# Products of the probabilities with v in 512 columns, once per head and sequence, from one generation of transposed probabilities

## The chip, the core and the metric

The kernel runs on one core of a Trainium2 chip. A core has a matrix engine (TensorE, "PE" in the profile; its loads of stationary operands are shown apart as "PEld"), a vector engine ("DVE"), a scalar engine ("ACT"), a general engine ("POOL") and a sync engine ("SP") that issues the DMAs between device memory and on-chip memory. On-chip memory is SBUF (operands) and PSUM (banks of 128 x 512 32-bit numbers, into which TensorE writes). Each engine works off its own list of instructions in order, and waits on semaphores for the others. The metric is the time of one execution in microseconds (us) on the device; lower is better. A result is the median of several runs.

## The reference, cut to what matters

An encoder layer over two sequences of 512 tokens (a "prompt" and a "sample"), with 1024 features. Three branches stand beside each other (a state-space scan, a differential attention, a cross attention to a memory), then gated merging, and a feed-forward part. The change lies in the differential attention. It has four heads; each head has two softmax maps over the same 512 keys, and their difference weights v:

```python
def _diff_attention(q, k, v, lam, subln_g, lambda_init):
    ...
    def block(qblk):
        s = jnp.einsum('bqhd,bkhd->bhqk', qblk, k).astype(jnp.float32) * scale
        probs = jax.nn.softmax(s, axis=-1).reshape(Bn, DIFF_HEADS, 2, Q_BLOCK, L)
        w = probs[:, :, 0] - lam * probs[:, :, 1]
        return jnp.einsum('bhqk,bkhe->bqhe', w.astype(v.dtype), v)

    o = lax.map(block, qb)
    o = o.transpose(1, 0, 2, 3, 4).reshape(Bn, L, DIFF_HEADS, DIFF_VDH)
    o = _rmsnorm(o, subln_g) * (1.0 - lambda_init)
    return o.reshape(Bn, L, DIFF_WIDTH)
```

All of it is in 32-bit floating point.

## The kernel before, in words

**Halves.** A product of two 32-bit matrices is made from reduced-precision halves: `split` (lines 131 to 139) writes the high half with a copy on ACT (line 134 or 137) and the low half, the remainder, on DVE (line 135 or 138). A product then takes three matmuls: high by high, low by high, high by low.

**The attention phase** (lines 736 to 940) goes through 32 steps. A step is a head h (0 to 3), a sequence s (0 or 1) and a block qt of 128 queries (0 to 3), in this nesting, so four steps in a row share h and s. The loop (lines 919 to 933) has an index i; its iteration i does, in the order in which TensorE gets it:

- if i is odd, `scores(i + 1)`: the two maps of steps i+1 and i+2. For each of the two steps, six matmuls on TensorE make two banks; DVE takes the row maxima (line 543, tile `nb`), ACT the exponentials (line 548, tile `e`), and DVE combines the two maps into `e0` (lines 552, 864, 865);
- `fill(10)`: some ten matmuls of other work (filler, below);
- `turn(i)`: TensorE transposes the four 128 x 128 blocks of `e0` into one bank of the pool `tr` (line 875; line 69 in the profile, `bktr<-ident,e`), ACT writes the high half `pH` (line 134), DVE the low half `pL` (line 135);
- if step i-1 has an odd qt, `outputs(i - 1)`: the product of v with the transposed probabilities of two query blocks, 12 matmuls of 256 columns into one half of a bank of the pool `oo` (lines 891 to 893). After the second half of a head and sequence, ACT copies the bank to `osb` (line 896);
- `fill(10)` again;
- two iterations after the last block of a head and sequence, `squares`: TensorE transposes `osb`, ACT squares and sums rows (line 907); three iterations after it, `normed`: `factor` takes a root on ACT (line 198) and a reciprocal on DVE (line 199, tile `rs`), TensorE spreads the factors (line 202; line 69 in the profile, `bktr<-ident,rs`), DVE scales `osb` (line 915) and SP stores it.

Below, "turn k" is the call of `turn` for step k, and "outputs k" the call of `outputs` that follows step k.

**Filler.** `fill` takes units from a queue of generators: projections of the layer's input to q, k, v and gates (tiles `xh`, `xl`, `wh`, `wl`), and towards the end the products of the merging (`yh`, `yl`). Their banks (pool `mm`, two of them) are emptied by DVE (lines 752 and 754 for q and k, line 797 for the merging), or by ACT (line 632 for gates). The gates are stored to device memory (`gD`) and loaded again (`gl`); the other branches' outputs come from `bD` into `yt`, and are split into `yh` and `yl`.

**Buffers.** The pool `tr` has two PSUM banks, shared in turn by one bank of `scores`, by `turn`, by `squares` and by `normed`; the pool `sc` has three, the pool `oo` one. `pT` has four slots of 128 x 4 x 256: two generations of `pH` and `pL`, each for two query blocks.

**What sets the order.** On TensorE the attention phase keeps the order in which the code is written (`PE.on = True`, line 687). On the other engines the framework's scheduler places the instructions by its own estimates, so that a change in the code can move rows there too.

Of the kernel before, what the change touches and what calls it, by code (L numbers as in the profile page):

```python
# [10 lines left out]
F32 = mybir.dt.float32  # L11
F32R = mybir.dt.float32r
# [7 lines left out]
P = 128  # L20
L = 512
# [51 lines left out]
def encoder(ctx: ExitStack, tc: tile.TileContext, a, out):  # L73
    nc = tc.nc
    V, S, PO, PE = nc.vector, nc.scalar, nc.gpsimd, InOrder(tc, nc.tensor)
# [8 lines left out]
    rp = ctx.enter_context(tc.tile_pool(name="rp", bufs=2))  # L84
# [3 lines left out]
    def open_tags(es, side=None, **tags):  # L88

        for tag, n in tags.items():  # L90
            pools[tag] = es.enter_context(tc.tile_pool(name=tag, bufs=n, side=side, reuse_waits="tile"))
# [10 lines left out]
    xp_es, phase = ExitStack(), ExitStack()  # L102
# [3 lines left out]
    def slot(tag, shape=(P, NT), dt=F32, name="sl"):  # L106
        return pools[tag].tile(list(shape), dt, tag=tag, name=name)

    def bank(tag="mm"):
        return pools[tag].tile([P, 512], F32, tag=tag, name="bk" + tag)  # L110

    def aux():
        return bank("tr")
# [17 lines left out]
    def split(hi, lo, src, scale=None):  # L131

        if scale is None:
            h = S.copy(hi, src)  # L134
            l_ = V.tensor_tensor(out=lo, in0=src, in1=hi.bitcast(F32), op=ALU.subtract)  # L135
        else:
            h = S.activation(out=hi, in_=src, func=AF.Copy, scale=scale)
            l_ = V.scalar_tensor_tensor(out=lo, in0=src, scalar=scale, in1=hi.bitcast(F32), op0=ALU.mult, op1=ALU.subtract)
        return h, l_
# [210 lines left out]
    with yielding(last_s):  # L350
        x_norm(0, norm[0], range(5, 8))
        _, bc = factor(ss1, DM)
# [245 lines left out]
    def fill(n):  # L598
        nonlocal owed
        owed += n  # L600
        while owed > 0 and queue:
            r = next(queue[0], None)
            if r is None:
                queue.pop(0)
            else:
                owed -= r
        if not queue:
            owed = 0

    def finish(g):  # L610
        while any(g is g_ for g_ in queue):
            fill(1)
# [75 lines left out]
    steps = [(h, s, lt) for h in range(4) for s in range(NS) for lt in range(4)]  # L688
    es, pT = {}, {}
    AHEAD = 2  # L690
    for i in range(-AHEAD, len(steps) + 1):
        if i + AHEAD < len(steps):
            h, s, lt = steps[i + AHEAD]
# [12 lines left out]
        if 0 <= i < len(steps):  # L706
            h, s, lt = steps[i]
# [3 lines left out]
            tr = aux()  # L711
# [4 lines left out]
        if i > 0 and steps[i - 1][2] == 3:  # L716
            h, s, _ = steps[i - 1]
            pTh, pTl = pT.pop((h, s))
            oo = bank("oo")
# [5 lines left out]
            osb = xa.tile([P, L], F32, tag="osb", name="xosb", bufs=1)  # L725
# [7 lines left out]
    phase.close()  # L733


    open_tags(phase, v2=2, qk=12, pT=4)
    aes = ExitStack()
    ap_ = aes.enter_context(tc.tile_pool(name="att", bufs=2, reuse_waits="tile"))
    acol = aes.enter_context(tc.tile_pool(name="acol", bufs=2, reuse_waits="tile"))
# [21 lines left out]
    qk = {}  # L761
# [48 lines left out]
    def first_in():  # L810
        b0.append(merge_in(0, ["qk", "qk", "qk", "v"]))
        yield 0
# [31 lines left out]
    s0, ss, osb = {}, {}, {}  # L844
# [22 lines left out]

    def turn(i):
        h, s, qt = steps[i]
        if qt % 2 == 0:  # L870
            pT[h, s, qt // 2] = tuple(slot("pT", [P, 4, 2 * P], F32R, n_) for n_ in ("pH", "pL"))
        e0 = es.pop(i)
        tr = aux()
        for j in range(4):
            PE.transpose(tr[:, j * P : (j + 1) * P], e0[:, j * P : (j + 1) * P], ident)
        ps = slice(qt % 2 * P, qt % 2 * P + P)
        split(*(p_[:, :, ps] for p_ in pT[h, s, qt // 2]), tr.rearrange("p (j q) -> p j q", j=4))

    def outputs(i):

        h, s, qt = steps[i]
        if h == 2 and s == qt - 1 == 0:
            finish(v1_)
        vh, vl = (v1 if h >= 2 else v0)[s]
        vs = slice((h % 2) * P, (h % 2) * P + P)
        pH, pL = pT.pop((h, s, qt // 2))
        if qt == 1:
            osb[h, s] = bank("oo")
        od = osb[h, s][:, qt // 2 * 2 * P : (qt // 2 + 1) * 2 * P]
        for j in range(4):  # L890
            PE.matmul(od, vh[:, j, vs], pH[:, j, :], start=(j == 0), stop=False)
            PE.matmul(od, vh[:, j, vs], pL[:, j, :], start=False, stop=False)
            PE.matmul(od, vl[:, j, vs], pH[:, j, :], start=False, stop=(j == 3))
        if qt == 3:
            o_ = rp.tile([P, L], F32, tag="nsq", name="osb", bufs=2)
            S.copy(o_, osb[h, s])
            osb[h, s] = o_

    def squares(i):
        h, s, _ = steps[i]  # L900
# [17 lines left out]
    n = len(steps)  # L918
    for i in range(-1, n + 3):
        if i % 2 and i + 1 < n:  # L920
            scores(i + 1)
        if i == 22:
            queue.insert(1, first_in())
        fill(10 if i < n - 1 else 16)
        if 0 <= i < n:
            turn(i)
        if 0 < i <= n and steps[i - 1][2] % 2:
            outputs(i - 1)
        fill(10)
        if 1 < i <= n + 1 and steps[i - 2][2] == 3:  # L930
            squares(i - 2)
        if i > 2 and steps[i - 3][2] == 3:
            normed(i - 3)
# [218 lines left out]
    for i in range(KFF):  # L1152
# [14 lines left out]
        ps = products(i, w)  # L1167
        p0 = next(ps)
        if i == 0:
            for s in range(NS):  # L1170
                _, bc = rstd(accs[s], DM)
# [92 lines left out]
    for v, (m, lo_, hi_) in enumerate(VISITS):  # L1264
        ps = [bank() for _ in range(6)] + [aux()]
# [22 lines left out]
        ps = iter(ps)  # L1288
# [523 lines left out]
```

## Time and profile before

| what | value |
|---|---|
| median of 3 runs | 1598.01 us (1597.61 to 1598.38) |
| the profiled execution's own time | 1596.6 us |
| its span, first to last instruction | 1594.5 us |
| TensorE busy | 1576.7 us, 99% of the span, 7838 matmuls |
| DVE, ACT, POOL busy | 1161.4, 630.9, 531.5 us (73%, 40%, 33%) |
| attention phase, first to last turn | 529.36 to 744.42 us |
| matmuls of 128 x 256 in `outputs` | 192 (three groups of 64) |

A row of the timeline gives the start in us from the span's start, the duration in us, the engine, the line, the operation, the tiles written and read, and in brackets how long the engine had stood idle before it and for whom. Matmuls overlap: each shows a duration longer than the distance to the next, so the cost of one is the distance from its start to the next one's start. A line of the profile can be that of a helper: all matmuls show line 66, all transposes line 69, all high halves line 134 or 137 and all low halves line 135 or 138.

### The profile page before, as it was taken

How to read it: one execution, taken by the hardware profiler on the slowest of the kernel's cores; microseconds unless marked ns; L12 is line 12 of the kernel's file. 1: busy time of each engine (PE TensorE's matmuls, PEld its weight loads, DVE VectorE, ACT ScalarE, POOL GpSimd, SP SyncE). 2: the span in 40 equal slices, each digit the busy share in tenths (PEclk: the TensorE clock that was granted, in tenths of full speed). 3: DMA queues.
4: the chain of work that ended last, by engine and by line, in shares of the span. 5: the costliest groups of instructions: out<-in, count | busy, mean ns of one | idle time of the engine just before them, and what ended most of it. 6: DMA issues, size and time to landing. Idle time of an engine off the chain costs nothing.

```text
span 1594.5 us, 21527 instructions
## 1 busy us (share of the span) xinstructions
PE 1576.7 (99%) x7838; PEld 1316.7 (83%) x7838; DVE 1161.4 (73%) x1857; ACT 630.9 (40%) x1114; POOL 531.5 (33%) x434
## 2 busy tenths in 40 slices
PE   9999999999999999999999999999999999999997
PEld 7888888888898889878888888888888888788877
DVE  7978995076774766775545578888898778988664
ACT  6644213265552465573223443323333233233323
POOL 0010000001333221300443357666665553444553
PEclk9999999999999999999999999999999999999999
DMA  9553623675762111254543432333332223986222
GB/s 364 177 167 119 213 93 114 180 267 206 264 225 102 43 57 40 73 174 143 197 144 122 144 108 92 119 126 125 119 119 106 84 89 116 345 333 196 85 67 106
DMA packets 104890, 237.84 MB, mean 149 GB/s; under 512 B 13520, under 2 KB 45008, under 8 KB 104784
## 3 DMA queue, kind: packets, MB, share of 16 engines
q1 hardware_dynamic: 104784, 236.47, 43.6%
q8 instruction: 61, 1.00, 0.3%
q14 instruction: 45, 0.37, 0.1%
HBM read 165.16 MB, written 71.27 MB: 148 GB/s over the span
## 4 chain that ended last, share of the span: by engine, by line
PE 85%; DVE 5%; DMA 3%; issue 2%; POOL 2%; SPq 1%; ACT 1%; POOLq 0%; DVEq 0%; ACTq 0%
PE bkmm L66 74%; PE bktr L66 3%; PE bkoo L66 2%; DVE tl L135 2%; PE bktr L69 2%; PE bksc L66 1%; PE bktr L1646 1%; DMA wf<-in_w_in 0%; PE bktr L1583 0%; PE bktr L1707 0%; PE bktr L1706 0%; PE bktr L1705 0%; DVE wl L135 0%; SPq L1633 0%; DMA mt<-in_memT 0%
## 5 line engine op out<-in xcount | busy, mean ns | idle before, releaser
L66 PE MATMUL bkmm<-xh,wh 128*128 128x512 f32 x640 | 254.4, 398 | 0.0
L66 PE MATMUL bkmm<-xl,wh 128*128 128x512 f32 x640 | 250.3, 391 | 0.0
L66 PE MATMUL bkmm<-xh,wl 128*128 128x512 f32 x640 | 250.2, 391 | 0.0
L66 PE MATMUL bkmm<-th,wl 128*128 128x512 f32 (+1 forms) x621 | 241.1, 389 | 1.7 <-DVE wl L135 1.7
L66 PE MATMUL bkmm<-tl,wh 128*128 128x512 f32 (+1 forms) x621 | 241.0, 388 | 0.0
L66 PE MATMUL bkmm<-th,wh 128*128 128x512 f32 (+1 forms) x621 | 240.7, 388 | 0.0
L134 ACT CAST wh<-wf 128x1024 fp32r<-128x1024 f32 (+1 forms) x134 | 118.0, 880 | 211.2 <-PE bkmm L66 181.9
L135 DVE TENSOR_TENSOR wl<-wf,wh 128x1024 fp32r<-128x1024 f32 (+1 forms) x134 | 148.6, 1109 | 58.9 <-ACT wh L134 54.0
L66 PE MATMUL bkmm<-th,w 128*128 128x512 f32 x432 | 141.6, 392 | 3.3 <-DVE up L1119 1.5
L66 PEld LDWEIGHTS bkmm<-xh,wl 128*128 128x128 f32 x640 | 120.2, 188 | 26.3 <-issue 0.4
L66 PEld LDWEIGHTS bkmm<-xh,wh 128*128 128x128 f32 x640 | 120.3, 188 | 26.1 <-issue 3.2
L66 PEld LDWEIGHTS bkmm<-xl,wh 128*128 128x128 f32 x640 | 120.4, 188 | 22.3 <-issue 0.2
L66 PEld LDWEIGHTS bkmm<-th,wl 128*128 128x128 f32 x621 | 116.5, 188 | 26.5 <-DVE wl L135 2.7
L66 PEld LDWEIGHTS bkmm<-th,wh 128*128 128x128 f32 x621 | 116.6, 188 | 23.9
L66 PEld LDWEIGHTS bkmm<-tl,wh 128*128 128x128 f32 x621 | 116.6, 188 | 23.8
L454 POOL TENSOR_TENSOR raw<-raw 128x128 f32<-128x128 f32 x28 | 15.1, 540 | 307.0 <-DVE nb L545 228.9
L1183 POOL TENSOR_TENSOR up<-up,acc 128x512 f32<-128x512 f32 x44 | 84.1, 1930 | 84.2 <-DVE up L1119 84.2
L66 PEld LDWEIGHTS bkmm<-th,w 128*128 128x128 f32 x432 | 80.9, 188 | 24.9 <-DVE up L1119 4.8
L801 POOL TENSOR_TENSOR mg<-mg,gl 128x1024 f32<-128x1024 f32 x16 | 43.8, 2740 | 138.9 <-DVE gl L797 134.3
L66 PE MATMUL bkmm<-tl,w 128*128 128x512 f32 x216 | 84.2, 390 | 0.0
L1182 ACT ACTIVATE ac<-gf 128x512 f32<-128x512 f32 x44 | 27.8, 633 | 126.6 <-DMA aD<-ac 60.9
L66 PE MATMUL bkmm<-yh,wh 128*128 128x512 f32 x192 | 76.1, 396 | 0.0
(652 smaller groups left out, 3558.8 us busy)
## 6 DMA issues: line engine op xcount, KB each, us to landing
wf<-in_w_in SPq DMA_DIRECT2D x40, 512.0 KB, 3.8
wD<-hl SPq DMA_DIRECT2D x28, 512.0 KB, 2.9
w<-wD SPq DMA_DIRECT2D x28, 512.0 KB, 5.0
gD<-gt SPq DMA_DIRECT2D x24, 512.0 KB, 2.8
gl<-gD SPq DMA_DIRECT2D x24, 512.0 KB, 3.3
wf<-in_w_fg SPq DMA_DIRECT2D x22, 512.0 KB, 3.6
wf<-in_w_fu SPq DMA_DIRECT2D x22, 512.0 KB, 3.7
aD<-ac SPq DMA_DIRECT2D x22, 512.0 KB, 2.9
```

The lines of the kernel that those rows point to most:

```text
L66: return self.put(self.eng.matmul(*args, **kw))
L69: return self.put(self.eng.transpose(*args, **kw))
L134: h = S.copy(hi, src)
L135: l_ = V.tensor_tensor(out=lo, in0=src, in1=hi.bitcast(F32), op=ALU.subtract)
L454: PO.tensor_tensor(out=a22, in0=a21, in1=a22, op=ALU.add)
L801: PO.tensor_tensor(out=mg[m], in0=mg[m], in1=gt, op=ALU.add)
L1182: last_t = S.activation(out=ac[:, cs], in_=gf, func=AF.Tanh, scale=0.5)
L1183: PO.tensor_tensor(out=up, in0=up, in1=accs[s], op=ALU.mult)
L1646: PE.matmul(ps[:, g * P : (g + 1) * P], w_[:, gg * P : (gg + 1) * P], u_[:, 8 * o + gg, :], start=True, stop=True)
```

## The change

`pT` gets two slots instead of four, each twice as wide (128 x 4 x 512): one generation of `pH` and `pL`, for all four query blocks of a head and sequence. The same SBUF is taken: four slots of 4 x 256 columns against two of 4 x 512. `turn` writes its 128 columns of it. `outputs` is called once per head and sequence, after the fourth block, with 12 matmuls of 512 columns; the bank of `oo` is taken and copied in the same call. And `outputs(i - 1)` stands ahead of `turn(i)` in the loop, which means that TensorE reads all of `pH` and `pL` before it transposes the next first block, whose halves go into the same slots.

```diff
-    open_tags(phase, v2=2, qk=12, pT=4)
+    open_tags(phase, v2=2, qk=12, pT=2)
...
     def turn(i):
         h, s, qt = steps[i]
-        if qt % 2 == 0:
-            pT[h, s, qt // 2] = tuple(slot("pT", [P, 4, 2 * P], F32R, n_) for n_ in ("pH", "pL"))
+        if qt == 0:
+            pT[h, s] = tuple(slot("pT", [P, 4, L], F32R, n_) for n_ in ("pH", "pL"))
         e0 = es.pop(i)
         tr = aux()
         for j in range(4):
             PE.transpose(tr[:, j * P : (j + 1) * P], e0[:, j * P : (j + 1) * P], ident)
-        ps = slice(qt % 2 * P, qt % 2 * P + P)
-        split(*(p_[:, :, ps] for p_ in pT[h, s, qt // 2]), tr.rearrange("p (j q) -> p j q", j=4))
+        split(*(p_[:, :, qt * P : (qt + 1) * P] for p_ in pT[h, s]), tr.rearrange("p (j q) -> p j q", j=4))
 
     def outputs(i):
 
-        h, s, qt = steps[i]
-        if h == 2 and s == qt - 1 == 0:
+        h, s, _ = steps[i]
+        if h == 2 and s == 0:
             finish(v1_)
         vh, vl = (v1 if h >= 2 else v0)[s]
         vs = slice((h % 2) * P, (h % 2) * P + P)
-        pH, pL = pT.pop((h, s, qt // 2))
-        if qt == 1:
-            osb[h, s] = bank("oo")
-        od = osb[h, s][:, qt // 2 * 2 * P : (qt // 2 + 1) * 2 * P]
+        pH, pL = pT.pop((h, s))
+        od = bank("oo")
         for j in range(4):
             PE.matmul(od, vh[:, j, vs], pH[:, j, :], start=(j == 0), stop=False)
             PE.matmul(od, vh[:, j, vs], pL[:, j, :], start=False, stop=False)
             PE.matmul(od, vl[:, j, vs], pH[:, j, :], start=False, stop=(j == 3))
-        if qt == 3:
-            o_ = rp.tile([P, L], F32, tag="nsq", name="osb", bufs=2)
-            S.copy(o_, osb[h, s])
-            osb[h, s] = o_
+        osb[h, s] = rp.tile([P, L], F32, tag="nsq", name="osb", bufs=2)
+        S.copy(osb[h, s], od)
...
         fill(10 if i < n - 1 else 16)
+        if 0 < i <= n and steps[i - 1][2] == 3:
+            outputs(i - 1)
         if 0 <= i < n:
             turn(i)
-        if 0 < i <= n and steps[i - 1][2] % 2:
-            outputs(i - 1)
         fill(10)
```

In the built programs, TensorE's list is shorter by 96 matmuls, and POOL's order is the same. On DVE, ACT and SP all moved rows lie in the attention phase. Lines after 902 have numbers lower by five in the changed kernel (line 915 is line 910 there).

TensorE at iteration 12, where head 1 goes from its first sequence (steps 8 to 11) to its second, before: three matmuls of filler, the four transposes of turn 12 (`bktr<-ident,e`), then the first three of the twelve products of outputs 11.

```order
L66 MATMUL bkmm<-wh,xh_124 128x256
L66 MATMUL bkmm<-wl,xh_124 128x256
L66 MATMUL bkmm<-wh,xl_132 128x256
L69 MATMUL bktr<-ident,e 128x128 x4
L66 MATMUL bkoo<-pH,vh 128x256
L66 MATMUL bkoo<-pL,vh 128x256
L66 MATMUL bkoo<-pH,vl 128x256
```

The same place in the changed kernel: the last three of the twelve products of outputs 11, then the transposes, then filler.

```order
L66 MATMUL bkoo<-pH,vh 128x512
L66 MATMUL bkoo<-pL,vh 128x512
L66 MATMUL bkoo<-pH,vl 128x512
L69 MATMUL bktr<-ident,e 128x128 x4
L66 MATMUL bkmm<-wh,xh_125 128x256
L66 MATMUL bkmm<-wl,xh_125 128x256
L66 MATMUL bkmm<-wh,xl_133 128x256
```

The products have gone ahead of the transposes; the twelve products that followed turn 10 are gone, and stand here in the doubled width.

DVE at the same iteration, before: the rest of the score work of steps 12 and 13 around the low half `pL` of turn 11.

```order
L135 TENSOR_TENSOR rl<-t_6091,rh 128x512
L552 RECIPROCAL r<-sm 128x1
L864 SCALAR_TENSOR_TENSOR r<-r,nlam,s_6109 128x1
L865 SCALAR_TENSOR_TENSOR e<-e,r 128x512
L552 RECIPROCAL r<-sm 128x1
L864 SCALAR_TENSOR_TENSOR r<-r,nlam,s_6109 128x1
L135 TENSOR_TENSOR pL<-bktr,pH 128x4x128
L865 SCALAR_TENSOR_TENSOR e<-e,r 128x512
```

DVE there in the changed kernel:

```order
L552 RECIPROCAL r<-sm 128x1
L864 SCALAR_TENSOR_TENSOR r<-r,nlam,s_6066 128x1
L135 TENSOR_TENSOR rl<-t_6048,rh 128x512
L865 SCALAR_TENSOR_TENSOR e<-e,r 128x512
L135 TENSOR_TENSOR pL<-bktr,pH 128x4x128
L552 RECIPROCAL r<-sm 128x1
L864 SCALAR_TENSOR_TENSOR r<-r,nlam,s_6066 128x1
L865 SCALAR_TENSOR_TENSOR e<-e,r 128x512
```

`pL` of turn 11 has moved ahead of two small instructions of step 13.

DVE between iterations 26 and 27, before: low halves of the merging's inputs (`yl`), an emptying of a filler bank (line 797), and the scaling of `osb` of head 2's second sequence (line 915).

```order
L138 SCALAR_TENSOR_TENSOR yl_7430<-yt,yh_7429 128x1024
L138 SCALAR_TENSOR_TENSOR yl_7436<-yt,yh_7435 128x1024
L797 SCALAR_TENSOR_TENSOR mg_7326<-gl,bkmm 128x512
L138 SCALAR_TENSOR_TENSOR yl_7442<-yt,yh_7441 128x1024
L915 SCALAR_TENSOR_TENSOR osb<-osb,g_3468,bktr 128x512
L543 TENSOR_REDUCE nb<-bktr 128x1
```

DVE there in the changed kernel:

```order
L138 SCALAR_TENSOR_TENSOR yl_7331<-yt,yh_7330 128x1024
L797 SCALAR_TENSOR_TENSOR mg_7227<-gl,bkmm 128x512
L138 SCALAR_TENSOR_TENSOR yl_7337<-yt,yh_7336 128x1024
L910 SCALAR_TENSOR_TENSOR osb<-osb,g_3468,bktr 128x512
L543 TENSOR_REDUCE nb<-bktr 128x1
L138 SCALAR_TENSOR_TENSOR yl_7343<-yt,yh_7342 128x1024
```

The scaling of `osb` (and the first maximum of the next scores behind it) has moved ahead of the last `yl`, and the emptying ahead of the second.

## The prediction

> **What bounds the kernel now.** I read the page first, for which engine the end hangs on; then the busy time by stretches, for whether that holds in the attention phase too; then the waits of TensorE there; then the timeline around the products, for what a matmul really costs.
>
> ```profile
> span 1594.5 us, 21527 instructions
> PE 1576.7 (99%) x7838; PEld 1316.7 (83%) x7838; DVE 1161.4 (73%) x1857; ACT 630.9 (40%) x1114; POOL 531.5 (33%) x434
> ...
> PE 85%; DVE 5%; DMA 3%; issue 2%; POOL 2%; SPq 1%; ACT 1%; POOLq 0%; DVEq 0%; ACTq 0%
> ```
>
> TensorE is busy for 99% of the span and carries 85% of the chain that ended last. In the attention phase it is fuller still:
>
> ```profile
> core 0: us, PE busy (x) PEld busy (x) DVE busy (x) ACT busy (x) POOL busy (x), PEclk, DMA share, GB/s
> 527.50:768.00 240.50, 239.64 (x1391) 199.09 (x1391) 167.47 (x314) 127.79 (x296) 37.91 (x25) 1.00 0.27 90
> ...
> PE bktr L69 <- DVE osb L915: 0.8, 1, 0.8
> ```
>
> Of 240.5 us it is idle for 0.86, and all but a trace of that is one wait, for the scaling of `osb` on DVE. The granted clock is 1.00. So time is saved here only where TensorE gets less to do or loses that wait, and lost only where the new order makes it wait. DVE is busy for 167 of the 240 us, but in bursts, and the low halves `pL` come from it.
>
> **The matmuls themselves.** TensorE overlaps its matmuls, so I take distances between starts. The first rows are outputs 1 (256 columns), the last two the first and the seventh start of a run in the cross attention (512 columns, the shape that the change gives the products, six of them).
>
> ```profile
> 541.65 0.60 PE L69 MATMUL bktr<-ident,e 128*128 128x128 f32 x4
> 542.00 0.36 PE L66 MATMUL bkoo<-pH,vh 128*128 128x256 f32 x1
> 542.21 0.28 PE L66 MATMUL bkoo<-pL,vh 128*128 128x256 f32 x1
> ...
> 543.39 0.28 PE L66 MATMUL bkoo<-pH,vl 128*128 128x256 f32 x1
> 543.51 0.40 PE L66 MATMUL bkmm<-xh,wh 128*128 128x512 f32 x1
> ...
> 493.55 0.39 PE L66 MATMUL bkoo<-xpTh,mkvh 128*128 128x512 f32 x1
> ...
> 494.91 0.39 PE L66 MATMUL bkmm<-xh,wh 128*128 128x512 f32 x1
> ```
>
> From 542.21 to 543.51 there are 11 distances: 0.1182 us each. From 493.55 to 494.91 there are six: 0.2267 us. So a matmul of 512 columns costs nearly two of 256. A head and sequence has 24 of the short ones now, 24 x 0.1182 = 2.84 us, and gets 12 of the long, 12 x 0.2267 = 2.72. That saves 0.12 us, and for eight heads and sequences 0.9 us. The first product after the transposes takes 0.21 instead of 0.12 (542.00 to 542.21); that surcharge isn't saved, since filler now follows the transposes and pays it. As a lower end, the filler of this phase steps by 0.229 (0.40 and 0.39 long as the row at 543.51); with that the saving is 24 x 0.1182 - 12 x 0.229 = 0.09, 0.7 us in all. I take 0.9, since the same pool `oo` and the same kind of operand stand in the rows that give it; ends 0.7 and 1.0.
>
> The copy of the bank on ACT, the evictions of the transposes and all DMAs stay in number and size; SBUF is the same. These I cost at nothing.
>
> **What the moved products do to the waits.** Two things move on TensorE. Outputs for the second block of each head and sequence go: 12 x 0.12 = 1.44 us less work between that turn and the fourth one, seven times in front of a next turn. And the full product stands ahead of the next turn instead of behind it, 0.35 us earlier. So the fourth block's `pL` must be ready 1.44 us sooner in clock time if DVE doesn't come along. Everything behind a product that waits is held: filler, turn, squares. How much lead is there? For each of the seven places I compare the end of the fourth `pL` with the start of the transposes behind which the product stands now, and which it replaces. The first, the two tightest and the last:
>
> ```profile
> 552.76 0.69 DVE L135 TENSOR_TENSOR pL<-bktr,pH 128x512 fp32r<-128x512 f32 x1
> 555.36 0.60 PE L69 MATMUL bktr<-ident,e 128*128 128x128 f32 x4
> ...
> 604.95 0.60 PE L69 MATMUL bktr<-ident,e 128*128 128x128 f32 x4
> 608.22 0.16 DVE L552 RECIPROCAL r<-sm 128x1 f32<-128x1 f32 x1
> 608.66 0.69 DVE L135 TENSOR_TENSOR pL<-bktr,pH 128x512 fp32r<-128x512 f32 x1
> 609.70 0.60 PE L69 MATMUL bktr<-ident,e 128*128 128x128 f32 x4
> ...
> 691.06 0.69 DVE L135 TENSOR_TENSOR pL<-bktr,pH 128x512 fp32r<-128x512 f32 x1
> 692.83 0.60 PE L69 MATMUL bktr<-ident,e 128*128 128x128 f32 x4
> ...
> 719.58 0.68 DVE L135 TENSOR_TENSOR pL<-bktr,pH 128x512 fp32r<-128x512 f32 x1
> 722.40 0.60 PE L69 MATMUL bktr<-ident,e 128*128 128x128 f32 x4
> ```
>
> The leads are 1.9 us (555.36 - 553.45), 0.35 (609.70 - 609.35), 1.1 (692.83 - 691.75) and 2.1 (722.40 - 720.26); the other three lie between 1.5 and 3.0. The second product is the first that reads `pL`, 0.23 us behind the first, so each place has that on top. Losing the full 1.44, only turn 11's place falls short, by 1.44 - 0.35 - 0.23 = 0.86, and turn 23's by about 0.1. Does DVE come along at turn 11?
>
> ```profile
> 599.50:609.30 9.80, 9.80 (x80) 8.96 (x79) 9.53 (x18) 6.61 (x14) 3.44 (x2) 1.00 0.24 80
> ```
>
> It does not: DVE works 9.53 of these 9.80 us, so this `pL` stays about where it is in clock time while TensorE arrives earlier. But DVE's new order puts it ahead of a reciprocal and its neighbour, worth 0.44 us (608.22 to 608.66). Left is 0.86 - 0.44 = 0.42, and with the 0.06 us that a signal took (the row of 716.22 below, against the end of line 915 at 716.16) 0.5 us. Ends: 0, if DVE's run gets shorter; 0.9, if the new order is worth nothing. At turn 23 the same small move covers the tenth; I take 0.
>
> [...]
>
> **The stall at 716 us.**
>
> ```profile
> 711.46 1.06 ACT L137 ACTIVATE yh<-yt 128x1024 fp32r<-128x1024 f32 x1 [1.60 <-DMA yt<-bD]
> 712.54 1.23 DVE L138 SCALAR_TENSOR_TENSOR yl<-yt,yh 128x1024 fp32r<-128x1024 f32 x1 [1.43 <-ACT yh L137]
> 713.69 0.68 DVE L797 SCALAR_TENSOR_TENSOR mg<-gl,bkmm 128x512 f32<-128x512 f32 x1
> 714.28 1.22 DVE L138 SCALAR_TENSOR_TENSOR yl<-yt,yh 128x1024 fp32r<-128x1024 f32 x1
> 715.42 0.74 DVE L915 SCALAR_TENSOR_TENSOR osb<-osb,g,bktr 128x512 f32<-128x512 f32 x1
> 716.22 0.66 PE L69 MATMUL bktr<-ident,e 128*128 128x128 f32 x4 [0.82 <-DVE osb L915]
> 716.63 0.48 PE L66 MATMUL bkmm<-yh,wh 128*128 128x512 f32 x1
> ```
>
> Turn 27 waits for a bank of `tr` that line 915 still reads, and line 915 stands on DVE behind a `yl` whose high half waited for the load `yt`. In the new order line 797 goes into the gap ahead of 712.54 and the last `yl` behind line 915, so line 915 can start when the `yl` of 712.54 is done, at 713.69, and end at 714.4. Without a wait turn 27 would start at 716.22 - 0.82 = 715.40 now, and 1.44 us earlier then, at 713.96, as outputs 25 is gone. Both shift alike by the 0.12 us of each sequence done, since the load hangs on a gate that TensorE computed. Wait: 714.43 + 0.06 - 713.96 = 0.5 instead of 0.82, a gain of 0.3. Ends: a gain of 0.8, if the load comes sooner; a loss of 0.4, if the load stays put while TensorE is ahead by 0.7.
>
> **Other waits that come nearer.** The factors `rs` are asked for by `normed` behind the products of the second block, so this lead shrinks by 1.44 too. The tightest of the seven:
>
> ```profile
> 652.74 1.28 ACT L198 ACT_TABLE_LOAD   x1
> 654.27 0.18 DVE L199 RECIPROCAL rs<-rs 128x4 f32<-128x4 f32 x1 [0.17 <-ACT rs L198]
> 656.12 0.60 PE L69 MATMUL bktr<-ident,rs 128*128 128x128 f32 x4
> ```
>
> Lead 656.12 - 654.45 = 1.67, left 0.2: no wait, cost 0. If ACT falls behind by one of its table loads (1.28 us in the rows of line 198) it is some 1.1 us here and at the first place, which has the same lead. The turns of the first blocks come later than now against their `e0`, and their banks: cost 0. On SP one store of `osb` goes ahead of one load `gl`; the loads run several units ahead, cost 0.
>
> **The sum.** -0.9 (matmuls) + 0.5 (wait for `pL` of turn 11) - 0.3 (stall at 716) = -0.7 us. The profiled execution took 1596.6 us, 2.1 more than its span, so this one would take 1595.9; the median of the runs shown is 1598.01, 1.4 above the profiled one, so the median I forecast is 1598.01 - 0.7 = 1597.3 us.
>
> **The rivals.**
>
> *Slower: the products wait for `pL` at most heads.* Now half of each product's operands are long ready, as the first two blocks' product is done early; then all 12 long matmuls hang on the last `pL`. For: DVE is in bursts of full work just there. Against: the leads above. It decides (3.2 us over the time before, which is 0.2%, about what a measurement of this kernel can tell from no change) if the waits sum to 3.2 + 0.9 = 4.1 us: with leads of 0.58, 1.3, 1.8, 1.8, 2.1, 2.4 and 3.2 (each with its 0.23), every `pL` would have to come 2.4 us later against TensorE, where 1.44 is what the change takes. Then 1601.2 or more. Chance 0.09.
>
> *Within 0.2%, but dearer:* both `rs` waits arise, 2.2 us: 1597.3 + 2.2 = 1599.5. It counts to the forecast's side, and sets the upper end.
>
> *Faster: a matmul has a large fixed cost.* The four transposes take 0.35 us (541.65 to 542.00), 0.0875 per 128 columns. A column costs (0.2267 - 0.1182) / 256 = 0.42 ns, so 128 cost 0.054, and 0.033 us would be fixed. If the 96 matmuls that go each cost that, 3.2 us go; with the whole stall of 0.8 it is 1598.0 - 4.0 = 1594.0 us. Against: the same line through the two product sizes leaves 0.0097 us as fixed, from matmuls of the very kind. Chance 0.05. [...]
>
> *The change doesn't do what it says:* its program has the 96 matmuls less. I leave this out.
>
> **How the numbers follow.** The forecast, within 0.2% of before, has 0.86. Faster by more than that 0.05, slower 0.09, by the cases above. The range: at the low end the matmuls give 1.0, the stall goes (0.8), no `pL` waits, and the runs' spread of 0.4 comes on top: 1598.0 - 2.2 = 1595.8. At the high end the dearer case, 1599.5, with 0.3 of the spread: 1599.8.
>
> **What would show it right or wrong.** Right: 96 matmuls `bkoo<-pH` and `bkoo<-pL` of 128 x 512 at 0.227 us apart; one small wait of TensorE for `pL` near 608 us, under a microsecond, and none elsewhere; a stall for line 910 (915 now) near 714 us of about 0.5. The phase then ends some 0.7 us sooner, and nothing behind it changes. Wrong: waits of `bkoo` for `pL` at four or more places, waits of `bktr<-ident,rs` for line 199, or filler held for its banks by DVE; or else long products nearer to 0.20 us apart.

## The result, and the profile after

The changed kernel takes 1595.53 us, the median of 22 runs (1593.67 to 1597.04). The kernel before, in 22 runs beside them, takes 1597.61 (1595.65 to 1601.62). The ratio is 0.9986, with a 95% interval of 0.998 to 0.9991: 2.1 us faster, where 0.7 was forecast, and 0.27 us below the range. It stays within 0.2% of the kernel before, the case to which the forecast gave a chance of 0.86. Single executions of either kernel spread by 3 to 6 us, so one profiled execution tells little about the total, and a great deal about its stages.

Of the changed kernel's profiled execution (1596.49 us), the page says:

```profile
span 1594.7 us, 21337 instructions
PE 1575.4 (99%) x7742; PEld 1312.0 (82%) x7742; DVE 1164.0 (73%) x1857; ACT 629.7 (39%) x1114; POOL 535.2 (34%) x434
...
PE 87%; DVE 5%; DMA 2%; POOL 2%; issue 2%; ACT 1%; SPq 1%; POOLq 0%; ACTq 0%; DVEq 0%
```

There are 96 matmuls less, and TensorE is the bound as before. The span is 0.2 us longer than the one shown of before, although the median is 2.1 shorter. Two stages differ. The first row of each pair is the attention phase (first score matmul to last product of the probabilities with v); the second is the FFN output, the last product of the feed-forward part (first matmul of its tiles `th` with `w` to the last matmul). All these marks are starts of matmuls. Before:

```profile
core 0: us, PE busy (x) PEld busy (x) DVE busy (x) ACT busy (x) POOL busy (x), PEclk, DMA share, GB/s
520.84:751.66 230.82, 229.96 (x1348) 190.85 (x1348) 165.92 (x312) 127.14 (x292) 36.99 (x24) 1.00 0.26 88
1358.01:1587.20 229.19, 223.64 (x1080) 185.65 (x1078) 170.43 (x228) 72.79 (x118) 113.27 (x108) 1.00 0.53 188
```

After:

```profile
521.29:754.99 233.70, 230.30 (x1252) 187.09 (x1252) 167.07 (x312) 126.65 (x292) 37.29 (x24) 0.99 0.26 87
1361.34:1587.41 226.07, 222.50 (x1079) 186.02 (x1078) 169.10 (x227) 73.01 (x118) 112.99 (x108) 1.00 0.54 191
```

The stage that was changed got 2.9 us longer (230.82 to 233.70). A stage that starts 600 us behind it, and in which both programs have the same instructions in the same order on every engine, got 3.1 us shorter (229.19 to 226.07). The stretch between the two takes 606.35 us in both.

**The attention phase.** The waits of TensorE there, changed kernel:

```profile
PE bktr L69 <- DVE osb L910: 1.9, 1, 1.9
PE bktr L66 <- DVE pL L135: 1.5, 1, 1.5
```

The second was not there before. It stands at the first score matmul of step 24, which needs a bank of `tr` that `pL` of turn 22 still reads:

```profile
681.80 1.23 DVE L138 SCALAR_TENSOR_TENSOR yl<-yt,yh 128x1024 fp32r<-128x1024 f32 x1 [0.77 <-ACT yh L137]
682.94 0.68 DVE L135 TENSOR_TENSOR pL<-bktr,pH 128x512 fp32r<-128x512 f32 x1
683.68 0.49 PE L66 MATMUL bktr<-rh 64*128 64x512 f32 x1 [1.47 <-DVE pL L135]
```

Before, the same two rows stood so:

```profile
683.06 0.68 DVE L135 TENSOR_TENSOR pL<-bktr,pH 128x512 fp32r<-128x512 f32 x1
683.79 0.50 PE L66 MATMUL bktr<-rh 64*128 64x512 f32 x1
```

`pL` stands behind a `yl` that waits for its own high half, so it keeps its clock time; TensorE had come just in time, and comes 1.44 us sooner since the 12 products of outputs 21 are gone. It waits 1.47.

The other wait is the stall at 716 us, larger than before. In the changed kernel's profiled execution:

```profile
714.09 1.06 ACT L137 ACTIVATE yh<-yt 128x1024 fp32r<-128x1024 f32 x1 [2.67 <-DMA yt<-bD]
...
716.32 0.74 DVE L910 SCALAR_TENSOR_TENSOR osb<-osb,g,bktr 128x512 f32<-128x512 f32 x1
```

The load `yt` came late, and with it `yl` and line 910. TensorE starts again at 717.12. Then comes something of which the profile of before has nothing (two windows, before and behind the change of the clock; the granted clock is the column behind POOL's):

```profile
714.00:717.41 3.41, 1.48 (x9) 0.92 (x8) 2.23 (x3) 3.12 (x3) 0.00 (x0) 1.00 0.46 165
717.41:720.83 3.42, 3.42 (x12) 2.75 (x11) 3.42 (x6) 2.93 (x9) 0.00 (x0) 0.50 0.88 248
```

The granted clock is 0.50 behind the stall, and is back at 1.00 after 3.4 us. It costs 1.3 us, as the next table shows.

The products themselves, changed kernel, first of twelve and the transposes behind the twelfth:

```profile
724.66 0.39 PE L66 MATMUL bkoo<-pH,vh 128*128 128x512 f32 x1
...
727.40 0.38 PE L69 MATMUL bktr<-ident,e 128*128 128x128 f32 x2
```

That is 2.74 us for 12, 0.228 each, as forecast from the cross attention.

**All executions side by side.** Later runs (below) left the attention phase as it is in one of the two kernels; they serve as repeats of it. "Rest" is the length less the two waits.

| attention phase, us | length | wait at 684 | wait at 716 | rest |
|---|---|---|---|---|
| before | 230.82 | 0 | 0.82 | 230.00 |
| before, three repeats | 232.42, 231.13, 231.03 | 0 | 2.43, 1.12, 1.02 | 229.99, 230.01, 230.01 |
| after | 233.70 | 1.47 | 1.93 | 230.30 |
| after, repeat with halved clock | 233.70 | 1.47 | 1.95 | 230.28 |
| after, five repeats without | 230.99, 231.15, 230.97, 231.43, 232.05 | 1.46 to 1.47 | 0.50, 0.69, 0.49, 0.96, 1.55 | 229.01 to 229.04 |

So the edit itself is worth some 0.9 us in every execution: 1.0 by these marks (230.0 to 229.0), of which 0.1 belongs to the mark, since the last product, which it leaves out, takes 0.12 us before and 0.23 after. The wait at 684 costs 1.5 in every execution of the changed kernel; the wait at 716 goes with the load `yt` in both kernels, 1.35 us in the mean before and 1.15 after; and the halved clock costs 1.3 us where it comes, twice in seven. On the mean the phase got 0.6 us longer (231.35 to 232.0).

### The profile page after: what moved, and what is told of

The parts are those of the page before. It is cut to its first block, busy times and chain, and to the rows that moved or that the text cites. A ratio compares the mean times of both kernels' runs of the same rounds, so it can differ in the third digit from the quotient of the medians.

```text
span 1594.7 us, 21337 instructions
## 1 busy us (share of the span) xinstructions
PE 1575.4 (99%) x7742; PEld 1312.0 (82%) x7742; DVE 1164.0 (73%) x1857; ACT 629.7 (39%) x1114; POOL 535.2 (34%) x434
## 4 chain that ended last, share of the span: by engine, by line
PE 87%; DVE 5%; DMA 2%; POOL 2%; issue 2%; ACT 1%; SPq 1%; POOLq 0%; ACTq 0%; DVEq 0%
PE bkmm L66 76%; PE bktr L66 4%; PE bkoo L66 2%; PE bktr L69 2%; PE bksc L66 1%; DVE tl L135 1%; PE bktr L1641 1%; DVE wl L135 1%; DVE st L1659 0%; DMA wf<-in_w_in 0%; PE bktr L1578 0%; PE bktr L1702 0%; PE bktr L1701 0%; PE bktr L1700 0%; DMA mt<-in_memT 0%
## 5 line engine op out<-in xcount | busy, mean ns | idle before, releaser
L454 POOL TENSOR_TENSOR raw<-raw 128x128 f32<-128x128 f32 x28 | 15.1, 541 | 309.4 <-DVE nb L545 229.3
```

Of the source, the lines that this page charges most:

```text
L454: PO.tensor_tensor(out=a22, in0=a21, in1=a22, op=ALU.add)
```

## The experiments

### Both kernels again

The expectations speak of theory A: the matmuls give 0.9 us, and the waits near 680 to 730 us vary from execution to execution with the arrival of `yt`; and of theory B: what is left of the gain is there in every execution, in the matmuls (B1) or in the order (B2).

> The kernel before once more, for a second trace of it. Theory A (the median's gain of 2.1 us is 0.9 us of matmuls, and the rest is waits in the merging part of the attention phase, 680 to 730 us, that differ from execution to execution with the arrival of the loads yt): the attention phase shows another sum of waits of TensorE than the 0.8 us of the first trace, by 1 us or more, or a stretch of halved clock. Theory B (the rest of the gain is in every execution, in matmuls or order): the same waits to 0.3 us.

> The changed kernel once more, for a second trace of it. The first one showed waits of 1.5 us at 683.7 (first score matmul, for the pL of turn 22) and 1.9 us at 717.1 (turn 27, for line 910), and the clock halved from 717.6 to 720.8 us. Theory A: the wait at 717 and the halved clock come and go with the arrival of yt, the wait at 683.7 stays; here another sum, by 1 us or more. Theory B: the same waits to 0.3 us.

Measured, in one profiled execution each: the kernel before 1598.27 us, the changed one 1595.49. Attention phase 232.42 and 233.70; FFN output 229.3 and 225.9, where it was 229.2 and 226.1. So the wait at 716 does vary, as theory A has it, and the gain sits in the FFN output, where neither theory had looked. It comes again in the second pair, 3.4 us after 3.1: no chance event of one execution.

### The place without the width

Narrow products at the new place: everything as in the changed kernel, but each product is two times twelve matmuls of 256 columns.

```diff
-        for j in range(4):
-            PE.matmul(od, vh[:, j, vs], pH[:, j, :], start=(j == 0), stop=False)
+        for q in (slice(0, 2 * P), slice(2 * P, L)):
+            for j in range(4):
+                PE.matmul(od[:, q], vh[:, j, vs], pH[:, j, q], start=(j == 0), stop=False)
...
```

> Placement alone: outputs once per head and sequence, ahead of the turn, from one generation, but with 24 matmuls of 256 columns instead of 12 of 512. Theory A: 24 x 0.1182 = 2.84 us per group of products in place of 2.72, so 0.9 us slower than the changed kernel, about 1596.4 against 1597.6 before. Theory B1 (96 fewer matmuls save more than their distances show): about the time of before. Theory B2 (the gain is the placement's): the time of the changed kernel, 1595.5.

Measured: 1596.67 us (11 runs), ratio 1.000 (0.9991 to 1.0008) to a kernel before of 1596.53. So the place alone shows no gain, within 1.4 us either way. In the profile the attention phase takes 233.25 us with waits of 1.45 and 1.42, which leaves 230.4. Counted to the start of the matmul behind the last product, that is 0.4 more than before and 1.3 more than the changed kernel: the place costs 0.4, and at this place the width is worth 1.3, more than the 0.9 worked out from distances. The FFN output takes 227.8 us, 1.7 more than in the changed kernel. How much of that has to do with the width, this run does not tell.

The kernel before with its halves issued ahead of the turn:

```diff
         fill(10 if i < n - 1 else 16)
-        if 0 <= i < n:
-            turn(i)
         if 0 < i <= n and steps[i - 1][2] % 2:
             outputs(i - 1)
+        if 0 <= i < n:
+            turn(i)
```

> The kernel before with one edit: the products of a half (256 columns, two per head and sequence) are issued ahead of the turn they stood behind, so the place is moved and the width is not. Two phases are read: the attention phase from the first score matmul to the last product of the probabilities with v (before 230.8 and 232.4 us in two executions, after 233.7 in both) and the FFN output from the first matmul of its tiles th with w to the last matmul (before 229.2 and 229.3, after 226.1 and 225.9, the narrow products at the late place 227.8). If the place causes the shorter FFN output: about 226 there. If the length of TensorE's instruction stream causes it, which this edit leaves as it was: 228 to 229.5.

Measured: 1597.80 us in one execution, attention phase 233.44 us with waits of 0.37, 1.17 and 1.61 (230.3 without them, 0.3 more than before), FFN output 228.1. The place does not make the short FFN output. It is neither 226 nor 229, so a second cause was to be looked for.

### The length of TensorE's list

What differs between the two programs at 1360 us, if the instructions there are the same? TensorE's list is 192 instructions shorter up to that point, and the trace shows transfers of 16 KB on the queue for instructions (q8), some 29 us apart in this stage (61 in the whole program, of either kernel); they are taken here for pieces of TensorE's list. Idle products at the start shift them, as the table below shows, and leave every later instruction as it is:

```diff
     for _ in range(NWARM):
         PE.matmul(idle[:, :P], pad_r[:, :P], pad_r[:, :P], start=True, stop=True)
+    for _ in range(48):
+        PE.matmul(idle[:, :8], pad_r[:, :P], pad_r[:, :8], start=True, stop=True)
```

> The changed kernel with 48 idle products of 8 columns more at its very start, behind the 13 that stand there (two records each): TensorE's stream is as long again as that of the kernel before, and nothing else is changed. Theory F (the FFN output runs 3.2 us shorter because TensorE's stream is 96 matmuls and their loads shorter, so that its pieces are fetched at other moments): the FFN output takes 229 us again. Theory R (the FFN output's length follows from what stands in the attention phase, its places or its waits): 226 us, whatever stands at the start. The start itself gets some 2 to 5 us longer, which neither theory is read from.

> The changed kernel with 32 idle products of 8 columns more at its start (64 records and their loads, half a piece). Theory F: a third moment for the fetches, so the FFN output may take anything from 225 to 230 us, and other than in the runs with 48 or 64. Theory R: 226 us.

> The changed kernel with 64 idle products of 8 columns more at its start (128 records and as many loads, 256 instructions: at 64 bytes each, an estimate from the pieces of 16 KB that the trace shows about every 29 us, one whole piece). Theory F: the pieces fall where they fall in the changed kernel, and the FFN output takes 226 us. Theory R: 226 us too; what this run tells apart is whether a late start alone moves the phase, with the run that has 48.

And the reverse, the kernel before with 16 such products:

> The kernel before with 16 idle products of 8 columns more at its start: 32 records and as many loads, 64 instructions. The kernel before has 192 TensorE instructions more than the changed one, so with 64 more it is 256 ahead, which theory F counts as one whole fetched piece. So far, in the clock of the trace's transfers, the piece that comes near the FFN output's start begins 13 to 15 us ahead of its first matmul in every execution with a stream as long as before (before twice, both narrow versions, the padded one with 48), and there the first ts<-fb,fa of VectorE waits 0.25 to 0.61 us for the load of fb; in the changed kernel it begins 22 to 23 us ahead, and nothing waits. Theory F: the piece 22 to 23 us ahead, no wait of ts for fb, and an FFN output of 226 to 228 us. Theory R (what stands in the attention phase decides): the wait of 0.3 to 0.6 us stays, and the FFN output takes 229 us. The start gets about 4.5 us longer (8.97 us for 32 idle products in the run with 64 records, halved).

(By the windows of the profile the pieces lie 1 to 2 us further ahead than the expectation has them.) Measured: 1612.26, 1603.53, 1618.61 and 1602.08 us in one execution each; the start grew by 14.9, 9.0, 22.5 and 6.2 us, more than expected, with the granted clock at 0.50 there for 17.1, 13.7, 27.3 and 6.8 us; this is not what these runs were for. The FFN output took 229.5 us with 48, 226.7 with 32, 227.8 with 64, and 228.2 for the kernel before with 16. With 48, idle products at the start alone made the FFN output 3.4 us longer. But half of that is not what the kernel before has. Set against the changed kernel matmul by matmul, 1.8 us are lost in the first 14 us of the stage, and 1.6 behind them, where two waits of TensorE (1.04 and 0.83 us) are followed by a halved clock:

```profile
1386.15:1389.56 3.41, 1.54 (x6) 0.91 (x6) 3.41 (x6) 0.00 (x0) 0.29 (x1) 1.00 0.98 368
1389.56:1392.98 3.42, 3.42 (x10) 2.65 (x9) 3.42 (x4) 0.00 (x0) 3.42 (x3) 0.50 0.48 154
```

The kernel before has no such stretch there. That the run with 48 came out at 229 us, as theory F said, is therefore in part chance. Theory R falls for the first part of the stage, and for that only (see below the table). Theory F is right on what it says of the load; on the length it is wrong with 64 idle products, and just outside its 226 to 228 us in the kernel before with 16. The load first. The kernel before, transfers between 1343.5 and 1344.0 us (packets on the queue, MB, share of 16 engines in this half microsecond):

```profile
q8 instruction: 1, 0.02, 11.7%
```

11.7% of 16 engines for 0.5 us is one engine for 0.94 us. The load of `fb` runs from 1341.31 to 1346.0, and VectorE waits for it:

```profile
1346.00 0.69 DVE L989 TENSOR_TENSOR ts<-fb,fa 128x512 f32<-128x512 f32 x1 [0.50 <-DMA fb<-aD]
...
1368.68 1.68 POOL L1292 TENSOR_TENSOR y<-y,gf 128x512 f32<-128x512 f32 x1 [4.23 <-DVE gf L1119]
1369.13 1.78 DVE L1184 SCALAR_TENSOR_TENSOR ac<-ac,gf 128x512 f32<-128x512 f32 x1
1371.56 0.50 PE L66 MATMUL bkmm<-th,w 128*128 128x512 f32 x1 [1.05 <-DVE u L1119]
```

The changed kernel has its piece between 1337.0 and 1337.5, ahead of the load that is issued at 1344.63, and no wait:

```profile
1348.74 0.68 DVE L984 TENSOR_TENSOR ts<-fb,fa 128x512 f32<-128x512 f32 x1
...
1371.87 0.68 DVE L1179 SCALAR_TENSOR_TENSOR ac<-ac,gf 128x512 f32<-128x512 f32 x1
1371.99 1.71 POOL L1287 TENSOR_TENSOR y<-y,gf 128x512 f32<-128x512 f32 x1 [4.80 <-DVE ts L986]
```

And the kernel before with 16 idle products, whose piece lies between 1339.5 and 1340.0, 25 us ahead of the FFN output's first matmul (24 in the changed kernel):

```profile
1351.92 0.68 DVE L991 TENSOR_TENSOR ts<-fb,fa 128x512 f32<-128x512 f32 x1
...
1374.91 1.37 POOL L1294 TENSOR_TENSOR y<-y,gf 128x512 f32<-128x512 f32 x1 [4.54 <-DMA y<-x1D]
1375.05 1.78 DVE L1186 SCALAR_TENSOR_TENSOR ac<-ac,gf 128x512 f32<-128x512 f32 x1
```

The wait for `fb` is gone. But these rows show the second step. `ac<-ac,gf` takes 0.68 us when it starts ahead of GpSimd's add, or up to 0.02 us behind it, and 1.78 when the add has begun 0.14 us or more ahead: 1.1 us more, on an engine that is busy for all of this stage's first 20 us, and TensorE then waits for `u`. With 64 idle products it is the same: the piece lies 25 us ahead, nothing waits for `fb`, and the add comes first.

```profile
1391.61 1.67 POOL L1289 TENSOR_TENSOR y<-y,gf 128x512 f32<-128x512 f32 x1 [4.23 <-DVE gf L1116]
1392.05 1.78 DVE L1181 SCALAR_TENSOR_TENSOR ac<-ac,gf 128x512 f32<-128x512 f32 x1
```

In the kernel before the add ends at 1370.36, and `ac<-ac,gf` at 1370.91, 0.55 us behind it. It is 0.55 in the other two executions shown with the add first as well (1376.28 to 1376.83, and 1393.28 to 1393.83), though the add had begun 0.45, 0.14 and 0.44 us ahead. So in these rows its end goes with the end of the add.

All executions, by these two events:

| FFN output, us | add first (1.78) | `ac<-ac,gf` first (0.68) |
|---|---|---|
| piece 14 to 16 us ahead, `ts` waits 0.25 to 0.61 for `fb` | before 229.2; after with 48 idle products 229.5; narrow, new place 227.8 | before again 229.3; narrow, ahead of the turn 228.1 |
| piece elsewhere, no wait for `fb` | after with 64 idle 227.8; before with 16 idle 228.2; shifted filler, second time (below) 227.8 | after 226.1, 225.9, 226.4; shifted filler 226.5; after with 32 idle 226.7 |

Without either event it is 225.9 to 226.7 us, with one or both 227.8 to 229.5. That the piece meets the load and the wait follows holds in all 13, and idle products alone bring the wait or take it away. That the packets of `fb` queue behind the piece on one engine is argued from its position and its 0.94 us, not shown by itself. And the two events do not explain all: before again had 229.3 us without the add first.

What they do explain can be read off when each execution is set against the changed kernel's, matmul by matmul. In the first 18 us of the stage (the halved clock left out) nothing is lost without the events, 0.6 us with the late `fb` alone, 1.1 with the add first alone, and 1.5 to 1.8 with both, in all 13. In the kernel before that is 1.7 of the 3.1 us. The other 1.4 us are lost later, most of them 119 to 171 us into the stage. This later loss is 1.0 to 2.6 us in all four executions that issue the products twice per head and sequence (the kernel before twice, ahead of the turn, and with 16 idle products), and at most 0.7 in the nine that issue them once, the narrow ones among them. So, as far as 13 executions tell, it goes with the version of the attention phase, as theory R would have it, and not with the length of TensorE's list; how it comes about no run shows.

### GpSimd's adds left out

```diff
         for c_, t, s in ((c11, 0, 0), (c22, 4, 1), (c21, 4, 0), (c12, 0, 1)):
             yv = y[m + t][:, s * L : (s + 1) * L]
-            PO.tensor_tensor(out=yv, in0=yv, in1=c_, op=ALU.add)
+            if v:
+                PO.tensor_tensor(out=yv, in0=yv, in1=c_, op=ALU.add)
```

> The kernel before without GpSimd's four adds of the first visit of the FFN output (y<-y with gf, up and twice nsq; the output lacks these sums). Theory C: the FFN output's lengths differ in steps of 1.1 us because a scalar_tensor_tensor of VectorE (ac<-ac,gf) takes 1.78 us when GpSimd's add has begun ahead of it and 0.68 us when it has not, and a shift of 0.6 us decides which. Here both ac<-ac,gf near 1363 to 1370 us that had 1.78 us beside GpSimd: the second, which met the first y add, takes 0.68 us, TensorE's wait of 1.05 us for u is gone, and the FFN output takes 227.5 to 228.3 us instead of 229.2. Rival (the late load of fb makes u late by itself): the wait for u stays near 1 us, and the FFN output near 229 us.

> The changed kernel with the same four adds of the first visit left out. Theory C: ac<-ac,gf at that place took 0.68 us already, and only the split products tl<-fb,th and tl<-fa,th just behind it (2.30 and 1.77 us beside GpSimd's next adds) get shorter, so the FFN output takes 225.3 to 226.1 us, and the distance to the kernel before without these adds is about 2 us instead of 3.2. Rival: the distance stays 3.2 us.

Measured: 1596.47 and 1594.01 us. In the kernel before without these adds:

```profile
1369.03 0.68 DVE L1184 SCALAR_TENSOR_TENSOR ac<-ac,gf 128x512 f32<-128x512 f32 x1
```

It takes 0.68 us as theory C has it, and TensorE's wait for `u` is gone. The distance between the kernels' FFN outputs falls from 3.1 to 2.2 us (228.8 and 226.65). But both lengths lie above what was expected (227.5 to 228.3, and 225.3 to 226.1). In the kernel before, TensorE is 1.1 us sooner behind the place, and still 158 us into the stage; then it loses most of that again, the largest part by a wait of 0.64 us for a weight tile `w` at 162 us, which the execution with the adds does not have. The changed kernel gained nothing; its 226.65 lies 0.2 above the longest of its three executions. So the collision is real and costs 1.1 us at its place; by the whole stage the distance fell by 0.9. Of the 2.2 that stay, 0.6 go with the late `fb`, and the rest is the later loss, with waits that hang on loads.

### Other filler, and the changed kernel again

The new wait at 684 and the old one at 716 stand behind turns of third blocks. This version moves filler there from behind the first blocks:

```diff
-        fill(10)
+        fill(10 if not 0 <= i < n else (10, 10, 16, 10)[i % 4] if i < 4 else (4, 10, 16, 10)[i % 4])
```

> The changed kernel with filler shifted: six more filler matmuls behind each third block's turn (16 for 10), where the first half's products stood before, and six fewer behind the first block's turn (4 for 10). This gives DVE back the 1.4 us between the third block's turn and the next scores. Theory A: the wait of the scores for pL near 684 us goes, the one near 717 shrinks, and the halved clock with them; 0.5 to 2 us faster than the changed kernel, 1593.5 to 1595. Theory B: the time of the changed kernel to 0.5 us, the waits being outside of what sets the end.

Measured: 1593.88 us (11 runs) beside a kernel before of 1596.53, ratio 0.9985 (0.9976 to 0.9994). To set it against the changed kernel on one chip, both were run once more:

> The changed kernel again, timed on the same chip as the version with the filler shifted, so that the two can be set against each other. If the waits of the attention phase (1.5 and 1.9 us, with the halved clock behind the second) are in every execution: 1 to 2.5 us above the version with the filler shifted, and an attention phase of 233 to 234 us in the profile. If they come and go: no distance that the spread of single executions (2 us to either side) lets one see. The FFN output: 225.9 to 226.7 us, as in all executions so far with this stream.

> The version with the filler shifted (behind the third block 16 units instead of 10, behind the first 4 instead of 10 from the second head and sequence on), again. If the waits cost what the traces show: 1593 to 1594.5 us where the changed kernel has 1594.5 to 1596, and an attention phase of 231 to 232 us. Otherwise both within 0.5 us of each other.

Measured, beside a kernel before of 1597.10: the changed kernel 1595.46 (ratio 0.9989, 0.998 to 0.9998), the shifted filler 1594.04 (ratio 0.9979, 0.9969 to 0.9988). It is 1.4 us faster than the changed kernel; resampling both sets of runs puts that between 0.4 and 3.3. The waits of TensorE in the attention phase, changed kernel again, then shifted filler:

```profile
PE bktr L66 <- DVE pL L135: 1.5, 1, 1.5
PE bktr L69 <- DVE osb L910: 0.5, 1, 0.5
```

```profile
PE bktr L69 <- DVE osb L910: 0.9, 1, 0.9
PE bkoo L66 <- DVE pL L135: 0.7, 1, 0.7
```

The wait of 1.5 us at 684 is gone, and a product now waits 0.7 us for `pL` at 556. The expected lengths were half met: the changed kernel had 231.0 us where 233 to 234 were expected, since `yt` came in time and the clock stayed; the shifted filler has 232.0, with 1.4 us of filler more inside the phase (1258 matmuls against 1252) and 1.1 less behind it, up to the FFN output. So the wait at 684 belongs to every execution, and the halved clock does not. This version is faster than both kernels. What the traces show for it is 0.8 us in the attention phase, a wait of 0.7 in place of 1.5; the rest of the 1.4 they don't tell from spread.

## Why the prediction missed

**The matmuls, -0.9: right in size.** Measured -0.9 without the waits, at 0.228 us apart against 0.2267. That it fits so well is partly luck: by the narrow version it is made up of 0.4 that the new place costs, which the prediction put at nothing, and 1.3 that the width gives there.

**The wait for `pL` of turn 11, +0.5: wrong, it is 0.** The step that failed is that this `pL` "stays about where it is in clock time". Before, and then in the changed kernel:

```profile
602.22 1.98 DVE L135 TENSOR_TENSOR wl<-wf,wh 128x1024 fp32r<-128x1024 f32 x1
604.12 0.68 DVE L543 TENSOR_REDUCE nb<-bktr 128x1 f32<-128x512 f32 x1
```

```profile
601.22 1.22 DVE L135 TENSOR_TENSOR wl<-wf,wh 128x1024 fp32r<-128x1024 f32 x1
602.34 0.69 DVE L543 TENSOR_REDUCE nb<-bktr 128x1 f32<-128x512 f32 x1
...
606.90 0.69 DVE L135 TENSOR_TENSOR pL<-bktr,pH 128x512 fp32r<-128x512 f32 x1
...
608.52 0.40 PE L66 MATMUL bkoo<-pH,vh 128*128 128x512 f32 x1
```

VectorE is nearly as full as before in this stretch (9.21 of 9.80 us against 9.53), but `pL` comes 1.76 us sooner (608.66 to 606.90), and 2.2 sooner when counted from the start of the phase, where 0.44 were counted. The 0.44 of the new order are not what brings it: they go into a wait of 0.48 for `rh`. The whole burst runs sooner, by 1.78 us at its first maximum `nb` already (604.12 to 602.34). Ahead of that the scaling of `osb` has moved up, and `wl<-wf,wh` takes 1.22 us where it took 1.98. It is the pattern of `ac<-ac,gf`: before, GpSimd's `t<-t,rs` starts at 601.83, ahead of `wl`; in the changed kernel at 601.47, behind it. No run tests it at this place.

**The stall at 716, -0.3: neither shown nor refuted.** It is 0.5 to 1.95 us in seven executions after and 0.8 to 2.4 in four before, a mean gain of 0.2 that so few do not tell from nothing. The forecast took the profiled 0.82 for the stall's size; it was the smallest of the four, and `yt` decides. That a halved clock can follow a long one, as here behind 1.93 and 1.95 us, was not considered.

**The waits that come nearer, 0: wrong, +1.5.** The same 1.44 us that was taken off the leads of `pL` and of `rs` should have been taken off the lead of every bank of `tr` behind the second blocks, and one user of these banks, `scores`, was not looked at. Its lead at 683.79 was nothing, as the rows above show. This is a step left out, not one mis-sized.

**"Nothing behind it changes": wrong, -3.1.** This is the step that cost the prediction most. The instructions behind the phase did not change, but their times did. Of the 3.1 us, 1.7 go with the moment at which a piece of TensorE's list is fetched, with the load `fb` that comes late beside it, and with which of two engines starts first; idle products alone brought these on and took them away. The other 1.4 go with the version of the attention phase, and their cause stays open.

The sum of the measured parts is -0.9 + 1.5 - 0.2 + 0.4 (1.3 us in two of seven executions) - 3.1 = -2.3 us, against a median of -2.1. So the time fell, as forecast, for another reason: the attention phase, from which all of the 0.7 us was to come, got longer. The forecast of 1597.3 further stood on a median of three runs, 1598.01; with 22 runs the kernel before has 1597.61, 0.4 less. From there the same sum and the same ends would have taken in the result, with the same steps wrong. Of the rivals none came: no product waits for `pL`, no wait for `rs`, and no fixed cost per matmul at the distances (the narrow version at the new place is 1.3 us longer than the wide, where 96 times 33 ns would be 3.2).

## What to carry to other kernels

When a change takes work off the bounding engine at one place, take that time off the lead of every buffer which that engine asks for next, whoever fills it: the one that was just in time turns the gain into a wait of the same size (here 1.47 us for 1.44). Where a stage starts as this FFN output does, with VectorE busy for all of its first 20 us and a DMA share of 0.91 to 0.98 there, an edit far ahead can move it by 0.1% (here 1.8 us in its first 14, with 48 idle products) through nothing but when things happen, so compare stage by stage over several executions before a gain of that size is put down to the edit; a few idle instructions at the start are a cheap test of it, as long as the granted clock of the stage is looked at too. Put work that fills behind the turn that waits, not evenly.

## What was not expected of the hardware

- A difference of 0.1 us in who starts first, VectorE or GpSimd, goes with whether an instruction lasts 0.68 us or 1.78, in 13 of 13 executions; in the kernel before without GpSimd's adds it took 0.68.
- The load of one piece of TensorE's list, 16 KB on one engine for 0.9 to 1.5 us, goes with a data load that lands 0.25 to 0.6 us too late, and its moment moved with idle products at the start: in the changed kernel it lies 24 us ahead of the FFN output's first matmul, with 48 of them 14 to 16, with 64 of them 25.
- The clock went to 0.50 behind waits of 1.93 and 1.95 us, and stayed at 1.00 behind one of 2.43 (the kernel before, again). The trace shows what else tells: in each of the 15 executions all changes of the granted clock lie a whole number of 3.413 us apart (in the changed kernel 713.39 us, 209 times, before the halved window, and 866.99, 254 times, behind it), on a grid of windows that lies elsewhere in every execution (one starts at 714.00 us in the changed kernel, at 713.19 in the one below). The two windows shown for the changed kernel lie on this grid, and the wait of 1.93 falls into one of them. The wait of 2.43 falls into two, 1.43 and 1.00. These two are, in the kernel before, again:

```profile
713.19:716.60 3.41, 1.98 (x10) 1.05 (x6) 2.67 (x3) 3.05 (x3) 0.00 (x0) 1.00 0.54 170
716.60:720.02 3.42, 2.42 (x13) 2.07 (x14) 3.41 (x7) 1.84 (x5) 0.00 (x0) 1.00 0.81 222
```

Apart from the first 50 and the last 15 us of the program, three windows of all 15 executions have TensorE idle for 1.87 us or more, and exactly these three are followed by a window at 0.50 (the third is the one with 48 idle products); the next longest, 1.73 and 1.55 us, are not. Idle for 1.87 of its 3.41 us was enough in these executions; no run was made to find where the step lies.
